# The second matrix of FFN 1 by the seven-product block scheme that FFN 2 already uses

## The chip, the core and the metric

The kernel runs on one core of a Trainium2 chip. A core has five engines that run side by side, each with its own instruction list: TensorE (PE, the matrix multiplier), VectorE (DVE), ScalarE (ACT), GpSimd (POOL) and SyncE (SP, which issues most DMA transfers). They wait for one another by semaphores. An engine executes its list strictly in the order written, so an instruction that waits also holds up everything behind it in its own list.

The metric is device time in microseconds (us) of one execution. Before the change three runs took 1120.14, 1120.99 and 1121.80 us, so the median is 1120.99 us. The profiled execution took 1119.95 us, of which its trace covers a span of 1118.2 us.

## The reference

The function is one layer of a hybrid streaming encoder for 512 tokens of width 1024, in fp32. Reduced to what matters:

```python
def swiglu(x, w1, w3, w2):
    return (jax.nn.silu(x @ w1) * (x @ w3)) @ w2      # w1, w3: 1024 x 2816, w2: 2816 x 1024

f = swiglu(rms_norm(h, pre_g1), w1a, w3a, w2a)        # FFN 1
h = h + 0.5 * rms_norm(f, post_g1)
u = rms_norm(h, mix_pre_g)                            # feeds attention, RG-LRU and gates
...
h = h + rms_norm(merged @ w_o, mix_post_g)
f = swiglu(rms_norm(h, pre_g2), w1b, w3b, w2b)        # FFN 2
h = h + 0.5 * rms_norm(f, post_g2)
```

The hidden width 2816 is 22 tiles of 128. "w2a" is the second matrix of FFN 1 and "w2b" that of FFN 2; the work here is the two products `hidden @ w2`, 512 x 2816 by 2816 x 1024.

## The kernel before

**Precision.** Every fp32 product is made of three passes of the multiplier over rounded parts: high times high, low times high and high times low. `split2` makes the two parts of a tile: ACT copies it to the rounded type (`whi` or the first half of `hT`), and DVE subtracts that copy from the original (`wlo`). So each weight tile and each hidden tile costs an ACT copy and a DVE subtraction before PE can use it. For some tiles DVE is spared: ACT writes the negated original into `wlo` and a DMA issued by POOL adds the same weights from memory to it (an "accumulate DMA").

**The order of work** is written out by hand. The Python program emits instructions for all engines in one sequence, and each engine's list is its part of that sequence. Weights are loaded and split in the order of the list `order`; `get`, `dma_to` and `split_to` advance along it. `later` and `point` emit small pieces of work at chosen places between matmuls. SBUF is handed out in 42 slots of 128 x 1024 fp32, PSUM in eight banks.

**FFN, first half.** The first tiles of the hidden width (four in FFN 1, two in FFN 2) are made one by one; tiles 2 and 3 of FFN 1 (`kept`) are stored raw and finished later by `gate_kept` (a DVE multiplication by `Rb` and an ACT silu) and `swiglu_kept`. The rest goes through `Pairs.run`: a job makes two tiles of `x @ w1` or `x @ w3` by seven block products instead of eight, `a11, s1, s2, a12 (by c11), s4, s3, a22` (in the last job a12 comes behind s3), each of 12 matmuls of 256 columns (`mm_s`). Between them ACT copies partial results out of PSUM (`q1`, `q5`, `u`, `v`) and DVE adds them. The last product `a22` of a job is emitted inside the next job, by `last()`. It accumulates in the same bank `bu` from which `v` is copied, so it can begin only when ACT has made that copy. For a w1 job of FFN 1 `last()` also multiplies the result by `Rb` on DVE, and ACT then applies silu. Towards the end of the last job two calls of `tail()` prepare the first w2 tiles, and two hooks `late[end, 1]` and `late[end, 2]` can place more work behind its first and second product.

**FFN 1, second half** (`tok_gemm`). Before, `w2a` is a plain product. For 15 of the 22 tiles each weight tile is used for all four groups of 128 tokens (24 matmuls of 512 columns a tile); the last 7 tiles (`RF`) are kept and used group by group, so that the norm of one group of tokens (`norms`, `post_norm`) runs beside the matmuls of the next.

**FFN 2, second half** (`Halves`). Tiles 0 to 15 of `w2b` go through seven block products `m1, m5, m2, m6, m7, m3, m4`, each summed over four groups of four tiles: 28 units, each of 12 matmuls of 512 columns. `prep(n)` prepares the operands of a unit: ACT copies (`whi`, and `hx` or `uT`), DVE subtractions for the low parts, and `sums` (`T` on weights, `S` on hidden tiles, both DVE) for the next product. `run` calls `prep` five units ahead (`LEAD`) of the unit that it emits, then calls the hooks of that unit, then emits the matmuls, and at the end of a product emits `out`, which copies the product out of PSUM: on ACT for m1, m5 and m6, as an addition on DVE for m7. The banks `bu` are used in turn by m1, m6, m7 and m4, so m7 can begin only when ACT has copied m6 out. The first four units are prepared inside the last pair job, by the two hooks and the two calls of `tail()`. The remaining six tiles, 16 to 21, go group by group as in FFN 1, and `post_norm` adds the stored partial results (`part`) with one DVE addition for each. `LO_DMA` names the units whose low weights come by accumulate DMA: two of m1 (groups 2 and 3) and all of m2; m3 always has them that way.

Of the kernel before, what the change touches and what calls it, by code (L numbers as in the profile page):

```python
# [15 lines left out]
P = 128  # L16
# [35 lines left out]
def hybrid_layer(ctx: ExitStack, tc: tile.TileContext, a: dict, out: bass.AP):  # L52
# [48 lines left out]

    order = []

    def want(name, n, first=0):
        order.extend((name, i) for i in range(first, n))

    paired = set()

# [6 lines left out]
            order.extend([(na, i), (na, i + 1), (nb, i), (nb, i + 1)])  # L115

    want_ffn("w1a", "w3a", NC1)
    want("w2a", FT)
    order += [("xr", i) for i in range(8)]
    order += [("wg", i) for i in range(8)]  # L120
    order += [("wk", 0), ("wk", 1), ("wv", 0), ("wv", 1)]
# [8 lines left out]
    paired.update(range(len(order), len(order) + 16 - WGP))  # L130
    order += [("wg", i) for i in range(WGP, 16)]
    order += [("wao", i) for i in range(8)]
    want("wo", 8)
    want_ffn("w1b", "w3b", NC2)
    want("w2b", FT, SF)

    st = {"dma": 0, "split": 0, "get": 0}
    raws, pairs = {}, {}
# [44 lines left out]
    def get(nm, i, ahead=2, rawahead=3):  # L183

        k = st["get"]
        assert order[k] == (nm, i), (order[k], nm, i)
        dma_to(k + 1 + ahead)
        split_to(k + 1 + ahead)
        dma_to(st["split"] + rawahead)
        st["get"] += 1  # L190
        return pairs.pop(k)
# [5 lines left out]
    def later(n, fn, rank=1):  # L197
        uid[0] += 1
        due.append((now[0] + n, rank, uid[0], fn))
# [36 lines left out]
    def mm_tok(acc, x, t, w, first, last, ns=(0, 1), skip=False):  # L236

        wh, wl = w
        c = slice(t * P, (t + 1) * P)
        for n in ns:  # L240
            s = slice(n * 512, (n + 1) * 512)
            pe.matmul(acc[n], x[:, 0, c], wh[:, s], start=first, stop=False, skip_group_check=skip)  # L242
            pe.matmul(acc[n], x[:, 0, c], wl[:, s], start=False, stop=False, skip_group_check=skip)  # L243
            pe.matmul(acc[n], x[:, 1, c], wh[:, s], start=False, stop=last, skip_group_check=skip)  # L244
# [66 lines left out]
            if after:  # L311
                after(n, c)

    def norms(acc, t, gpost, scale, gpre, spill, eps, mid=None):

        hg = slot([P, D], name="hg")
        junk = slot([P, D], name="junk")
        ss = small(2, "ss")
        rs = Rstd2()

        def half(n, c):
            act.activation(junk[:, c], h[t][:, c], AF.Square, accum_out=ss[:, n : n + 1])
            if n:
                rs.first(ss)
                dve.tensor_tensor(out=hg[:, c], in0=h[t][:, c], in1=gpre[:, c], op=ALU.mult)

        post_norm(acc, t, gpost, scale * NEWT, h[t], half, eps=eps, mid=mid)
        ht = h[t]
        if spill:
            sp.dma_start(out=h_scr[t], in_=h.pop(t))  # L330
        rs.root(ss)
        r = rs.value()
        dve.scalar_tensor_tensor(out=hg[:, :512], in0=ht[:, :512], scalar=r, in1=gpre[:, :512], op0=ALU.mult, op1=ALU.mult)
        act.activation(hg[:, 512:], hg[:, 512:], AF.Copy, scale=r)
        return hg
# [30 lines left out]
    def tok_gemm(nm, xs, n, R, gpost_name, scale, gpre_name, first, x_to=None, xf=None, spill=False, then=None, eps=None, pre=None):  # L366
# [8 lines left out]
        def accs(t):  # L375
            if t not in acc:
                acc[t] = [bank("acc"), bank("acc")]
            return acc[t]
# [21 lines left out]
                    if t % 2:  # L400
                        point()
        point(True)
        for k in range(F, n):
            x_to(k + 1)
            w[k] = get(nm, k, ahead=max(0, n - 1 - k), rawahead=2)
        gpost = bcast(gpost_name)
        gpre = bcast(gpre_name) if gpre_name else None
        if gpre_name:
# [4 lines left out]
        dma_to(st["split"] + 2)  # L413
        for t in range(NT):
            for ns in ((0,), (1,)):
                for k in range(F, n):
                    mm_tok(accs(t), xs[k], t, w[k], k == F if pre and t > 1 and ns == (1,) else k == 0, k == n - 1, ns, bool(pre))
            if not gpre_name:
                o = slot([P, D], name="o")

                def store(nn, c, t=t, o=o):
                    sp.dma_start(out=out[t * P : (t + 1) * P, c], in_=o[:, c])

                post_norm(acc[t], t, gpost, scale * NEWT, o, store, t == NT - 1, part=pre and pre.part(t))
                continue
            if t == NT - 1:
                break
            if t >= 1:
                trs[t - 1] = transpose_mm(us[t - 1])
            if t == NT - 2:  # L430

                transpose_out(trs[t - 1], t - 1)
            us[t] = norms(acc[t], t, gpost, scale, gpre, spill, ep(t))
            if t == 1:
                transpose_out(trs[t - 1], t - 1, xf)
        if not gpre_name:
# [16 lines left out]
        start(range(3))  # L453
        trs[t - 1] = transpose_mm(us[t - 1])
        mm_feat(bs[0], ws[0], 0, 256, ks=range(3, KT))
        us[t] = norms(acc[t], t, gpost, scale, gpre, spill, ep(t), between)
        transpose_out(trs[t - 1], t - 1, parts=(1,))
        transpose_xf(trs[t - 2], t - 2, xf, (1,))
        start()
# [30 lines left out]

    class Hidden:

        def __init__(self, block=0):
            self.f, self.t, self.done, self.block, self.eo = {}, {}, block, block, {}

        def place(self, f, own=None):

            if f >= self.block:
                return own
            g = f // 4  # L500
            if g not in self.eo:
                self.eo[g] = [slot([P, 2, SEQ], name="hEO") for _ in range(2)]
            return self.eo[g][f % 2][:, f // 2 % 2, :]

        def to(self, n):
            while self.done < n and self.done in self.f:
                hT = slot([P, 2, SEQ], F32R, name="hT")
                split2(hT[:, 0, :], hT[:, 1, :], self.f.pop(self.done))
                self.t[self.done] = hT
                self.done += 1  # L510

        def __getitem__(self, k):
# [2 lines left out]
    class Halves:  # L515
# [6 lines left out]

        def __init__(self, nm, hid, hooks):
            self.nm, self.hid, self.hooks = nm, hid, hooks
            self.gs = (1, 2, 3, 0)
            self.raw, self.ops, self.loaded, self.ready = {}, {}, 0, 0
            self.bank, self.c, self.accs, self.cast = {}, {}, {}, {}

# [104 lines left out]
        def run(self):  # L633
            for u in range(28):
                self.prep(u + LEAD)
                for fn in self.hooks.get(u, ()):
                    fn()
                self.unit(u)
                if u % 4 == 3 and self.NAMES[u // 4] in ("m1", "m5", "m6", "m7"):
                    later(0, lambda m=self.NAMES[u // 4]: self.out(m), 0)  # L640
                point()
            self.hid.eo.clear()
            for t in range(NT):
                n0 = self.bank["bc" if t < 2 else "bu"][t % 2]
                self.accs[t] = [n0, self.bank["bx"][t] if t < 2 else bank("acc")]
            self.bank.clear()

    QH = 4 * P

# [332 lines left out]
            load_x(2 * kp + 1)  # L982
    dma_to(NS + 2)

    hid, X1 = Hidden(), {}
    Rb = slot([P, 2, SEQ], name="Rb")
    pairs_a = Pairs(("w1a", "w3a"), NC1, FT, X1, hid, Rb)
    h_load([a["x"][t * P : (t + 1) * P, :] for t in range(NT)])
# [206 lines left out]
    for i in range(P // 16):  # L1195
        late[4 + i, 1] = [lambda i=i: bias_spread(i)]

    def w2_ahead():
        hid.to(hid.done + 1)
        split_to(st["split"] + 1)  # L1200

    pairs_a.run(w2_ahead, late)
    X1 = pairs_a = late = None
    for f in range(NG, NC1):
        later(1, lambda f=f: gate_kept(f))
        later(3, lambda f=f: swiglu_kept(f))
    later(10, softplus)
    xf = {(hh, th): slot([P, 4, 256], name="xf") for hh in range(2) for th in range(2)}
    bs = tok_gemm(
        "w2a", hid, FT, RF, "ffn1_post_g", 0.5, "mix_pre_g", [("xr", i) for i in range(4)], hid.to, xf=xf, spill=True, eps=veps)  # L1210
    hid = None


# [371 lines left out]
        mg.append(m)  # L1585


    hid, tn = Hidden(SF), []
    X2 = {"b11": uview(0, 0), "b21": uview(1, 0), "b22": uview(1, 1)}
    pairs_b = Pairs(("w1b", "w3b"), NC2, FT, X2, hid)  # L1590
    dma_one(pairs_b.k0)
# [27 lines left out]

    dve.tensor_tensor(out=tn[3], in0=xf[1, 0], in1=tn[1], op=ALU.subtract)  # L1620
    xf.clear()
    hid.f[0] = silu_mul(bs[0], bs[1], out=hid.place(0))
    X2["t3"] = to_slots(tn[2])
    hid.f[1] = silu_mul(bs[2], bs[3], out=hid.place(1))
    del bs
    late = {(0, 1): [lambda: X2.update(t4=to_uT(tn[3], 0, 1)), tn.clear]}
    pairs_b.prep(1, 1)

    def tail_tile(n):
        hid.to(n)  # L1630
        split_to(st["get"] + n - SF)

    def h_back(t):
        h[t] = slot([P, D], name="h")
        sp.dma_start(out=h[t], in_=h_scr[t])

    hooks = {u: [] for u in range(28)}
    for n, u in enumerate(RAW_TAIL):
        hooks[u].append(lambda n=n: dma_to(st["get"] + n + 1))
    for n, u in enumerate(SPLIT_TAIL):  # L1640
        hooks[u].append(lambda n=n: tail_tile(SF + n + 1))
    for t, u in enumerate(H_BACK):
        hooks[u].append(lambda t=t: h_back(t))
    half = Halves("w2b", hid, hooks)
    pairs_b.more = lambda n: half.load(LOAD_PAIRS[n])
    ahead = lambda: half.prep(half.ready + 1)
    end = len(pairs_b.jobs) - 1
    late[end, 1], late[end, 2] = [ahead], [ahead]
    pairs_b.run(ahead, late)
    X2 = pairs_b = None  # L1650
    tok_gemm("w2b", hid, FT, FT - SF, "ffn2_post_g", 0.5, None, [], hid.to, pre=half)


CONV_AT = (0, 1, 2, 4, 5, 6, 8, 10)
# [20 lines left out]
BY_DMA = {("wg", i) for i in range(2)}  # L1675

BY_POOL = {("wg", i) for i in range(2, 8)} | {("wk", 0), ("wk", 1)}
RF = 7

SF = 16  # L1680
LEAD = 5
U_SLOTS = 4
CAST_AT = 15
LO_DMA = {(m, i) for m in ("m1", "m2") for i in range(4)} - {("m1", 0), ("m1", 1)}
LOAD_PAIRS = (0, 4, 6, 8)
RAW_TAIL = (14, 16, 18, 20, 22, 24)
SPLIT_TAIL = (16, 18, 20, 22, 24, 26)
# [11 lines left out]
NG = 2  # L1699
# [55 lines left out]
```

## Time and profile before

| what | value |
|---|---|
| median of three runs | 1120.99 us (1120.14 to 1121.80) |
| profiled execution | 1119.95 us, span 1118.2 us |
| PE busy | 1107.4 us, 99 % of the span |
| DVE busy | 878.9 us, 79 % |
| ACT busy | 646.1 us, 58 % |
| `w2a` in FFN 1, plain | from 232.35 us to 353.9 us of the span |
| `w2b` blocks in FFN 2 | first matmul at 998.82 us |
| last matmul | starts at 1110.50 us |

All times inside the trace are counted from the start of the span. A timeline row gives the start, the duration, the engine, the line, the operation with what it writes and reads, and in brackets how long the engine was idle before it and what released it. Rows of the same kind that follow each other are joined ("x2"), and their duration is that of all together. A single matmul of 512 columns is listed with about 0.39 us because the rows include the pipeline's depth; consecutive ones start about 0.23 us apart, and that distance is what counts. The same holds for DVE and ACT: a row's start to the next row's start is what an instruction costs in a full queue. The granted clock (PEclk) is the share of full speed that the chip allowed the multiplier.

### The profile page before, as it was taken

What the parts mean: (1) busy time and instruction counts of PE and PEld (TensorE: products, weight loads), DVE (VectorE), ACT (ScalarE), POOL (GpSimd) and SP (SyncE); (2) the same over time, 40 slices, a digit from 0 to 9 for tenths busy, and PEclk for the clock granted to TensorE, in tenths of its full rate; (3) what the DMA queues carried; (4) which work ended last, traced back from release to release, by engine and by line L of the source; (5) the groups of instructions that cost most, each with busy time, mean ns of one, the idle gap of its engine ahead of it and who ended that gap; (6) DMA issues with size and microseconds to landing.
All of it is one profiled execution on the core that took longest, in us unless ns stands there. A gap on an engine that the chain in (4) does not pass through costs nothing.

```text
span 1118.2 us, 17951 instructions
## 1 busy us (share of the span) xinstructions
PE 1107.4 (99%) x6898; PEld 998.9 (89%) x6898; DVE 878.9 (79%) x1279; ACT 646.1 (58%) x1143; POOL 380.1 (34%) x298
## 2 busy tenths in 40 slices
PE   9999999999999999999999999999999999999997
PEld 7899999988888877899888888888999999997885
DVE  5899989887437978888678867767889899789944
ACT  7755555574326687756656564456455555577721
POOL 0044344200101523223556573010976665502100
PEclk9999999999999999999999999999999999999999
DMA  9226563264313553147223245342332323487732
GB/s 346 96 89 146 123 148 114 76 221 155 113 57 115 156 144 107 45 151 245 76 76 94 92 155 208 136 185 94 114 89 102 114 77 113 149 227 157 198 118 76
DMA packets 47319, 148.06 MB, mean 132 GB/s; under 512 B 5233, under 2 KB 7153, under 8 KB 47233
## 3 DMA queue, kind: packets, MB, share of 16 engines
q1 hardware_dynamic: 39632, 127.47, 33.7%
q0 software_dynamic: 7312, 18.92, 8.6%
q8 instruction: 54, 0.88, 0.3%
q10 hardware_dynamic: 288, 0.52, 0.2%
q14 instruction: 33, 0.26, 0.1%
HBM read 131.18 MB, written 13.62 MB: 129 GB/s over the span
## 4 chain that ended last, share of the span: by engine, by line
PE 98%; DMA 2%; DVE 0%; issue 0%; ACT 0%; DVEq 0%; SPq 0%; ACTq 0%
PE c L657 13%; PE c L658 13%; PE c L659 13%; PE f L224 9%; PE f L225 9%; PE f L226 9%; PE acc L243 5%; PE acc L242 5%; PE acc L244 5%; PE hw L613 2%; PE hw L614 2%; PE hw L612 2%; DMA wlo<-in_w2b_dram 1%; PE pt L1496 1%; PE hw L244 1%; PE hw L243 1%
## 5 line engine op out<-in xcount | busy, mean ns | idle before, releaser
L658 PE MATMUL c<-uT,wlo 128*128 128x256 f32 x516 | 146.0, 283 | 0.0
L659 PE MATMUL c<-uT,whi 128*128 128x256 f32 x516 | 146.0, 283 | 0.0
L657 PE MATMUL c<-uT,whi 128*128 128x256 f32 x516 | 146.0, 283 | 0.0
L658 PE MATMUL c<-Xh,wlo 128*128 128x256 f32 x504 | 142.7, 283 | 0.0
L657 PE MATMUL c<-Xh,whi 128*128 128x256 f32 x504 | 142.7, 283 | 0.0
L224 PE MATMUL f<-uT,whi 128*128 128x512 f32 (+1 forms) x368 | 136.4, 371 | 0.0
L225 PE MATMUL f<-uT,wlo 128*128 128x512 f32 (+1 forms) x368 | 134.8, 366 | 0.0
L226 PE MATMUL f<-uT,whi 128*128 128x512 f32 (+1 forms) x368 | 134.8, 366 | 0.0
L659 PE MATMUL c<-Xl,whi 128*128 128x256 f32 x456 | 129.0, 283 | 0.0
L214 DVE TENSOR_TENSOR wlo<-S,whi 128x1024 fp32r<-128x1024 f32 x86 | 120.1, 1396 | 6.5 <-POOL OL L1532 3.1
L213 ACT ACTIVATE whi<-S 128x1024 fp32r<-128x1024 f32 x86 | 88.3, 1054 | 23.1 <-DVE S L706 22.0
L658 PEld LDWEIGHTS c<-uT,wlo 128*128 128x128 f32 x516 | 99.0, 192 | 0.2
L657 PEld LDWEIGHTS c<-uT,whi 128*128 128x128 f32 x516 | 99.0, 192 | 0.2
L659 PEld LDWEIGHTS c<-uT,whi 128*128 128x128 f32 x516 | 99.0, 192 | 0.0
L657 PEld LDWEIGHTS c<-Xh,whi 128*128 128x128 f32 x504 | 96.8, 192 | 0.3 <-issue 0.3
L658 PEld LDWEIGHTS c<-Xh,wlo 128*128 128x128 f32 x504 | 96.7, 192 | 0.1
L659 PEld LDWEIGHTS c<-Xl,whi 128*128 128x128 f32 x456 | 87.5, 192 | 0.0
L224 PEld LDWEIGHTS f<-uT,whi 128*128 128x128 f32 x368 | 69.4, 189 | 12.5 <-issue 1.7
L226 PEld LDWEIGHTS f<-uT,whi 128*128 128x128 f32 x368 | 69.4, 188 | 11.4
L225 PEld LDWEIGHTS f<-uT,wlo 128*128 128x128 f32 x368 | 69.4, 189 | 10.8
L1480 POOL TENSOR_SCALAR P<-P,d 128x256 f32<-128x256 f32 (+1 forms) x64 | 62.5, 991 | 45.2 <-DVE d L1478 25.3
L242 PE MATMUL acc<-whi,hT 128*128 128x512 f32 x188 | 73.3, 390 | 0.0
(429 smaller groups left out, 3139.8 us busy)
## 6 DMA issues: line engine op xcount, KB each, us to landing
raw_w2a<-in_w2a_dram SPq DMA_DIRECT2D x22, 512.0 KB, 4.0
raw_w1b<-in_w1b_dram SPq DMA_DIRECT2D x22, 512.0 KB, 4.3
raw_w3b<-in_w3b_dram SPq DMA_DIRECT2D x22, 512.0 KB, 4.4
raw_w2b<-in_w2b_dram SPq DMA_DIRECT2D x22, 512.0 KB, 5.8
raw_w3a<-in_w3a_dram SPq DMA_DIRECT2D x21, 512.0 KB, 4.5
raw_w1a<-in_w1a_dram SPq DMA_DIRECT2D x20, 512.0 KB, 4.3
raw_wg<-in_wg_dram SPq DMA_DIRECT2D x16, 512.0 KB, 3.9
wlo<-in_w2b_dram POOLq DMA_DIRECT2D x10, 512.0 KB, 6.9
```

Of the source, the lines that this page charges most:

```text
L213: act.activation(hi, src, AF.Copy)
L214: dve.tensor_tensor(out=lo, in0=src, in1=f32(hi), op=ALU.subtract)
L224: pe.matmul(ps[:, c0:c1], wh[:, s], h_, start=k == 0 and c0 == 0, stop=False, skip_group_check=True)
L225: pe.matmul(ps[:, c0:c1], wl[:, s], h_, start=False, stop=False, skip_group_check=True)
L226: pe.matmul(ps[:, c0:c1], wh[:, s], l_, start=False, stop=k == KT - 1, skip_group_check=True)
L242: pe.matmul(acc[n], x[:, 0, c], wh[:, s], start=first, stop=False, skip_group_check=skip)
L243: pe.matmul(acc[n], x[:, 0, c], wl[:, s], start=False, stop=False, skip_group_check=skip)
L244: pe.matmul(acc[n], x[:, 1, c], wh[:, s], start=False, stop=last, skip_group_check=skip)
L657: pe.matmul(ps, wh[:, s], xh, start=first, stop=False, skip_group_check=True)
L658: pe.matmul(ps, wl[:, s], xh, start=False, stop=False, skip_group_check=True)
L659: pe.matmul(ps, wh[:, s], xl, start=False, stop=k == 3, skip_group_check=True)
L1480: pool.tensor_scalar(out=pt[:, x, b0:256], in0=pt[:, x, b0:256], scalar1=d[:, x : x + 1], scalar2=None, op0=ALU.mult)
```

## The change

`w2a` is now made by the same block scheme, and the setting up of that scheme moves from FFN 2 into a function `blocks` that both call. In both FFNs the 16 tiles in blocks are 4 to 19 (`gs = (1, 2, 3, 4)`), and the six others are `TAIL`. `LO_DMA` keeps only m2, so all low parts of m1 are now subtractions on DVE, in both FFNs. Three things of FFN 1 are fitted in: the gates of the two kept tiles become hooks of units 15, 17, 18 and 19 and stand first among the hooks of their unit; `softplus` becomes a hook of unit 25; and the residual `h`, so far held in four slots throughout FFN 1, is dropped and loaded again from `x` during the units named by `H_BACK`. `norms` passes the partial results on to `post_norm`. In FFN 2 tiles 0 and 1 go to a slot of their own.

```diff
-    want("w2a", FT)
+    want("w2a", TAIL)
...
-    want("w2b", FT, SF)
+    want("w2b", TAIL)
...
-            us[t] = norms(acc[t], t, gpost, scale, gpre, spill, ep(t))
+            us[t] = norms(acc[t], t, gpost, scale, gpre, spill, ep(t), part=pre and pre.part(t))
...
-            self.gs = (1, 2, 3, 0)
+            self.gs = (1, 2, 3, 4)
...
+    def blocks(nm, hid, pairs, late, h_src):
+
+        hooks = {u: [] for u in range(28)}
+
+        def tail_tile(n):
+            hid.to(n + 1)
+            split_to(st["get"] + n + 1)
+
+        def h_back(t):
+            h[t] = slot([P, D], name="h")
+            sp.dma_start(out=h[t], in_=h_src(t))
+
+        for at_, fn in ((RAW_TAIL, lambda n: dma_to(st["get"] + n + 1)), (SPLIT_TAIL, tail_tile), (H_BACK, h_back)):
+            for n, u in enumerate(at_):
+                hooks[u].append(lambda n=n, fn=fn: fn(n))
+        half = Halves(nm, hid, hooks)
+        pairs.more = lambda n: half.load(LOAD_PAIRS[n])
+        ahead = lambda: half.prep(half.ready + 1)
+        end = len(pairs.jobs) - 1
+        late[end, 1], late[end, 2] = [ahead], [ahead]
+        pairs.run(ahead, late)
+        return half
...
-    def w2_ahead():
-        hid.to(hid.done + 1)
-        split_to(st["split"] + 1)
-
-    pairs_a.run(w2_ahead, late)
+    h.clear()
+    half = blocks("w2a", hid, pairs_a, late, lambda t: a["x"][t * P : (t + 1) * P, :])
     X1 = pairs_a = late = None
-    for f in range(NG, NC1):
-        later(1, lambda f=f: gate_kept(f))
-        later(3, lambda f=f: swiglu_kept(f))
-    later(10, softplus)
+    for u, fn in zip(KEPT_AT, (gate_kept, swiglu_kept) * (NC1 - NG)):
+        half.hooks[u].insert(0, lambda f=NG + KEPT_AT.index(u) // 2, fn=fn: fn(f))
+    half.hooks[SOFTPLUS_AT].append(softplus)
...
-    tok_gemm("w2b", hid, FT, FT - SF, "ffn2_post_g", 0.5, None, [], hid.to, pre=half)
+    half = blocks("w2b", hid, pairs_b, late, lambda t: h_scr[t])
+    X2 = pairs_b = None
+    tok_gemm("w2b", hid, FT, len(TAIL), "ffn2_post_g", 0.5, None, [], pre=half)
...
-RF = 7
-
-SF = 16
+
+TAIL = (0, 1, 2, 3, 20, 21)
+KEPT_AT = (15, 17, 18, 19)
+SOFTPLUS_AT = 25
...
-LO_DMA = {(m, i) for m in ("m1", "m2") for i in range(4)} - {("m1", 0), ("m1", 1)}
+LO_DMA = {("m2", i) for i in range(4)}
```

More of the change, by code (lines that the diff above doesn't have):

```diff
@@ L102, in hybrid_layer, with want @@
     order = []
-    def want(name, n, first=0):
-        order.extend((name, i) for i in range(first, n))
+    def want(name, tiles):
+        order.extend((name, i) for i in tiles)
     paired = set()
@@ L132, in hybrid_layer @@
     order += [("wao", i) for i in range(8)]
-    want("wo", 8)
+    want("wo", range(8))
     want_ffn("w1b", "w3b", NC2)
-    want("w2b", FT, SF)
+    want("w2b", TAIL)
     st = {"dma": 0, "split": 0, "get": 0}
@@ L312, in post_norm, with norms @@
                 after(n, c)
-    def norms(acc, t, gpost, scale, gpre, spill, eps, mid=None):
+    def norms(acc, t, gpost, scale, gpre, spill, eps, mid=None, part=None):
         hg = slot([P, D], name="hg")
@@ L325, in half @@
                 dve.tensor_tensor(out=hg[:, c], in0=h[t][:, c], in1=gpre[:, c], op=ALU.mult)
-        post_norm(acc, t, gpost, scale * NEWT, h[t], half, eps=eps, mid=mid)
+        post_norm(acc, t, gpost, scale * NEWT, h[t], half, eps=eps, mid=mid, part=part)
         ht = h[t]
@@ L402, in tok_gemm @@
         point(True)
-        for k in range(F, n):
-            x_to(k + 1)
-            w[k] = get(nm, k, ahead=max(0, n - 1 - k), rawahead=2)
+        tail = list(pre.hid.seq) if pre else list(range(F, n))
+        for i, k in enumerate(tail):
+            x_to(F + i + 1)
+            w[k] = get(nm, k, ahead=max(0, len(tail) - 1 - i), rawahead=2)
         gpost = bcast(gpost_name)
@@ L415, in tok_gemm @@
             for ns in ((0,), (1,)):
-                for k in range(F, n):
-                    mm_tok(accs(t), xs[k], t, w[k], k == F if pre and t > 1 and ns == (1,) else k == 0, k == n - 1, ns, bool(pre))
+                for k in tail:
+                    new = k == tail[0] and (t > 1 and ns == (1,) if pre else k == 0)
+                    mm_tok(accs(t), xs[k], t, w[k], new, k == tail[-1], ns, bool(pre))
             if not gpre_name:
@@ L455, in tok_gemm @@
         mm_feat(bs[0], ws[0], 0, 256, ks=range(3, KT))
-        us[t] = norms(acc[t], t, gpost, scale, gpre, spill, ep(t), between)
+        us[t] = norms(acc[t], t, gpost, scale, gpre, spill, ep(t), between, pre and pre.part(t))
         transpose_out(trs[t - 1], t - 1, parts=(1,))
@@ L491, in hybrid_layer, with __init__ @@
     class Hidden:
-        def __init__(self, block=0):
-            self.f, self.t, self.done, self.block, self.eo = {}, {}, block, block, {}
+        def __init__(self, seq):
+            self.seq, self.f, self.t, self.done, self.eo = seq, {}, {}, 0, {}
         def place(self, f, own=None):
-            if f >= self.block:
+            if f in self.seq:
                 return own
@@ L505, in to @@
         def to(self, n):
-            while self.done < n and self.done in self.f:
+            while self.done < min(n, len(self.seq)) and self.seq[self.done] in self.f:
+                k = self.seq[self.done]
                 hT = slot([P, 2, SEQ], F32R, name="hT")
-                split2(hT[:, 0, :], hT[:, 1, :], self.f.pop(self.done))
-                self.t[self.done] = hT
+                split2(hT[:, 0, :], hT[:, 1, :], self.f.pop(k))
+                self.t[k] = hT
                 self.done += 1
@@ L983, in hybrid_layer @@
     dma_to(NS + 2)
-    hid, X1 = Hidden(), {}
+    hid, X1 = Hidden(TAIL), {}
     Rb = slot([P, 2, SEQ], name="Rb")
@@ L1196, in hybrid_layer @@
         late[4 + i, 1] = [lambda i=i: bias_spread(i)]
-    def w2_ahead():
-        hid.to(hid.done + 1)
-        split_to(st["split"] + 1)
-    pairs_a.run(w2_ahead, late)
+    h.clear()
+    half = blocks("w2a", hid, pairs_a, late, lambda t: a["x"][t * P : (t + 1) * P, :])
     X1 = pairs_a = late = None
-    for f in range(NG, NC1):
-        later(1, lambda f=f: gate_kept(f))
-        later(3, lambda f=f: swiglu_kept(f))
-    later(10, softplus)
+    for u, fn in zip(KEPT_AT, (gate_kept, swiglu_kept) * (NC1 - NG)):
+        half.hooks[u].insert(0, lambda f=NG + KEPT_AT.index(u) // 2, fn=fn: fn(f))
+    half.hooks[SOFTPLUS_AT].append(softplus)
     xf = {(hh, th): slot([P, 4, 256], name="xf") for hh in range(2) for th in range(2)}
     bs = tok_gemm(
-        "w2a", hid, FT, RF, "ffn1_post_g", 0.5, "mix_pre_g", [("xr", i) for i in range(4)], hid.to, xf=xf, spill=True, eps=veps)
+        "w2a", hid, FT, len(TAIL), "ffn1_post_g", 0.5, "mix_pre_g", [("xr", i) for i in range(4)], xf=xf, spill=True, eps=veps, pre=half)
+    half = None
     hid = None
@@ L1585, in mg_out @@
         mg.append(m)
-    hid, tn = Hidden(SF), []
+    hid, tn = Hidden(TAIL), []
     X2 = {"b11": uview(0, 0), "b21": uview(1, 0), "b22": uview(1, 1)}
@@ L1621, in hybrid_layer @@
     xf.clear()
-    hid.f[0] = silu_mul(bs[0], bs[1], out=hid.place(0))
+    t01 = slot([P, 2, SEQ], name="sw")
+    hid.f[0] = silu_mul(bs[0], bs[1], out=t01[:, 0, :])
     X2["t3"] = to_slots(tn[2])
-    hid.f[1] = silu_mul(bs[2], bs[3], out=hid.place(1))
+    hid.f[1] = silu_mul(bs[2], bs[3], out=t01[:, 1, :])
+    del t01
     del bs
@@ L1627, in hybrid_layer @@
     pairs_b.prep(1, 1)
[L1629 to L1649, printed above, removed]
+    half = blocks("w2b", hid, pairs_b, late, lambda t: h_scr[t])
     X2 = pairs_b = None
-    tok_gemm("w2b", hid, FT, FT - SF, "ffn2_post_g", 0.5, None, [], hid.to, pre=half)
+    tok_gemm("w2b", hid, FT, len(TAIL), "ffn2_post_g", 0.5, None, [], pre=half)
 CONV_AT = (0, 1, 2, 4, 5, 6, 8, 10)
```

## The prediction

> **What bounds the kernel now.** I read the page's busy shares and clock first, then PE's waits, then the timelines of the stages that the change touches.
>
> ```profile
> span 1118.2 us, 17951 instructions
> ...
> PE 1107.4 (99%) x6898; PEld 998.9 (89%) x6898; DVE 878.9 (79%) x1279; ACT 646.1 (58%) x1143; POOL 380.1 (34%) x298
> ...
> PEclk9999999999999999999999999999999999999999
> ```
>
> ```profile
> PE hw L613 <- DMA wlo<-in_w2b_dram: 2.0, 2, 1.1
> ```
>
> PE is busy 99% of the span at full clock and hardly waits; past its first microseconds its only waits are two on low weights in FFN 2's m1. A matmul removed is time saved, and every new wait of PE is time lost. Two things set the price of a matmul, and two the block scheme's pace. The chain that ended last shows the first:
>
> ```profile
> 334.06 0.23 PE acc L242
> ...
> 343.60 0.87 PE tr L343 x8
> ```
>
> Between these rows lie one group's 7 tail tiles x 2 halves x 3 = 42 matmuls of 512 columns: 9.54 / 42 = 0.227 us each, so a unit of 12 takes 2.73.
>
> **1. Matmuls removed.** Plain, 16 tiles of `w2a` take 16 x 24 = 384; in blocks 28 x 12 = 336. Saved: 48 x 0.227 = 10.9 us, all on PE's path. Tail: 6 x 24 in both.
>
> **2. The last pair job of FFN 1: a new wait (stall A).** PE, then ACT, then DVE there:
>
> ```profile
> 230.91 0.28 PE L657 MATMUL c<-Xh,w 128*128 128x256 f32 x1
> ...
> 232.35 0.40 PE L242 MATMUL acc<-whi,hT 128*128 128x512 f32 x1
> ```
> ```profile
> 225.35 0.38 ACT L796 ACTIVATE cc<-c 128x256 f32<-128x256 f32 x1 [1.06 <-PE c L659]
> 226.79 0.38 ACT L756 ACTIVATE ct<-c 128x256 f32<-128x256 f32 x1 [1.06 <-PE c L659]
> 227.07 1.05 ACT L798 ACTIVATE cc<-cc 128x1024 f32<-128x1024 f32 x1
> 228.02 0.62 ACT L213 ACTIVATE hT<-sw 128x512 fp32r<-128x512 f32 x1
> 228.54 1.05 ACT L178 ACTIVATE whi<-raw_w2a 128x1024 fp32r<-128x1024 f32 x1
> 229.67 0.39 ACT L778 ACTIVATE ct<-c 128x256 f32<-128x256 f32 x1
> ```
> ```profile
> 221.97 0.69 DVE L214 TENSOR_TENSOR w<-raw_w3a,w 128x512 fp32r<-128x512 f32 x1
> 225.77 1.23 DVE L797 TENSOR_TENSOR cc<-cc,Rb 128x1024 f32<-128x1024 f32 x1 [3.11 <-ACT cc L796]
> ```
>
> The hooks behind a11 and s1 now put units 0 and 1 on ACT and DVE, ahead of `last()`'s multiplication by Rb (L797). What a unit of m1 costs DVE is shown by FFN 2:
>
> ```profile
> 990.30 1.23 DVE L593 TENSOR_TENSOR wlo<-raw_w2b,whi 128x1024 fp32r<-128x1024 f32 x1 [1.17 <-ACT whi L588]
> 991.44 0.69 DVE L214 TENSOR_TENSOR hx<-hEO,hx 128x512 fp32r<-128x512 f32 x1
> 992.05 1.22 DVE L545 TENSOR_TENSOR raw_w2b<-raw_w2b,raw_w2b 128x1024 f32<-128x1024 f32 x1
> ...
> 993.78 1.22 DVE L593 TENSOR_TENSOR wlo<-raw_w2b,whi 128x1024 fp32r<-128x1024 f32 x1
> ```
>
> That is 993.78 - 990.30 = 3.48 us a unit, 1.14 for 1024 wide operations and 0.60 for 512. DVE begins unit 0 when its first copy, behind q1's, is there, about 223.8. Two units end at 230.8, and the multiplication at 232.0, where it used to end at 227.0. ACT's silu (L798) waits for it, and behind the silu in ACT's list stand unit 2's two copies (0.95 and 0.5 by the distances above) and only then the copy of `v` (L778): 232.1 + 0.95 + 0.95 + 0.5 = 234.5, done at 234.9. PE's last a22 accumulates into the bank that `v` is copied from, so it starts at 234.9, not 230.9. Stall A: 4.0 us. From the spread of the terms I allow 3.3 to 4.7. Before, the 3.11 us of DVE idle there covered the step.
>
> **3. DVE after that.** Unit 2 on DVE waits for its copy (234.1); units 2 and 3 and six small additions of the job end at 243.5, where unit 4 begins (234.1 + 2 x 3.48 + 2.4; four of the six take the 1.73 between the first two rows below, the other two 0.33 each). In FFN 2:
>
> ```profile
> 1002.60 0.41 DVE L767 TENSOR_TENSOR cc<-c,ct 128x256 f32<-128x256 f32 x1
> ...
> 1004.33 1.21 DVE L593 TENSOR_TENSOR wlo<-raw_w2b,whi 128x1024 fp32r<-128x1024 f32 x1
> ...
> 1048.44 0.69 DVE L214 TENSOR_TENSOR uT<-hEO,uT 128x512 fp32r<-128x512 f32 x1
> ```
> ```profile
> 1020.00:1040.00 20.00, 20.00 (x90) 16.54 (x89) 20.00 (x27) 14.98 (x21) 5.27 (x6) 1.00 0.84 189
> ```
>
> DVE (third of the busy columns) never rests there: 44.1 us from unit 4's first subtraction to the end of unit 19's `T`. In FFN 1 that ends at 243.5 + 44.1 = 287.6. PE starts unit 0 at 232.4 + 4.0 = 236.4 and would reach unit 16 at 236.4 + 16 x 2.73 = 280.0. By the same operations a unit of m5 costs DVE 3.48, of m2 and m6 2.34, of m7 2.87, which is 4 x 11.03 = 44.1 again; so counted, operands stay just ahead of PE up to unit 15, closest at unit 8 (0.2 us).
>
> **4. The kept gate at unit 15 (stall B).** These rows ran beside plain matmuls before:
>
> ```profile
> 237.16 1.28 DVE L1164 TENSOR_TENSOR kept<-kept,Rb 128x512 f32<-128x512 f32 x2
> ...
> 237.88 1.24 ACT L1165 ACTIVATE kept<-kept 128x512 f32<-128x512 f32 x2 [4.46 <-DVE kept L1164]
> ```
>
> (The second is ACT's.) Now the hook of unit 15 runs after `prep` of unit 19, so the DVE multiplication stands behind unit 19's `T`: 287.6 + 0.64 = 288.25. ACT's silu waits for it (0.62, to 288.9), and ACT's copy of m6 out of `bu` is emitted behind unit 15, thus behind that silu. Unit 16 (m7) begins in the same bank:
>
> ```profile
> 1044.48 1.28 ACT L626 ACTIVATE hc<-hw 128x512 f32<-128x512 f32 x2 [3.40 <-PE hw L614]
> ```
>
> In FFN 2 this copy waited for PE alone. In FFN 1 its first half ends near 289.5, 9.5 us after PE is ready. Lower end: with DVE as far ahead as in FFN 2 (1048.44 against m6's end near 1044.5 + 0.5), 3.4 + 0.64 + 0.62 + 0.64 = 5.3; upper 10.5. I take 9.5, the sum by this stage's own times. The gates at 18 and 19 meet a DVE that has then caught up: nothing.
>
> **5. The clock after stall B.**
>
> ```profile
> 1110.00:1111.00 1.00, 0.89 (x4) 0.39 (x3) 0.08 (x1) 0.00 (x0) 0.00 (x0) 1.00 0.00 0
> ...
> 1115.00:1116.00 1.00, 0.00 (x0) 0.00 (x0) 0.21 (x1) 0.00 (x0) 0.00 (x0) 0.91 0.73 280
> 1116.00:1118.20 2.20, 0.00 (x0) 0.00 (x0) 0.00 (x0) 0.00 (x0) 0.00 (x0) 0.50 0.32 111
> ```
> ```profile
> 1.10 4.21 PE L964 MATMUL w<-warm 128*128 128x256 f32 x18 [1.10 <-POOL warm L961]
> 5.63 0.80 PE L1014 MATMUL f<-uT,whi 128*128 128x512 f32 x1 [0.33 <-ACT uT L1007]
> ```
>
> After the last matmul (about 1110.9) the granted clock, the column before the DMA share, holds at 1.00 until about 1115.8 and is 0.50 from then: 4.9 us of idle. At the start 256-column matmuls come 4.21 / 18 = 0.234 us apart, twice the 0.12 of the pair jobs (1.44 for the 12 between the PE rows of part 2), and the slow pace lasts through the 0.80 matmul, to about 6.4: 5.3 us at half speed, 2.6 lost. Stall B, 9.5, is past 4.9, so PE should restart at half clock. The price lies between 0 (it holds) and 2.6; I take 2.6, the one restart shown. Stall A, 4.0, is short of it: 0.
>
> The Trainium skill ("TensorE: Matmul & The Clock Gate", Part 1: The HAM clock gate) says that the clock halves after at least one idle window of about 3.4 us and is restored after a busy one of the same length. That agrees with a drop seen after 4.9; by its window the restart would lose 3.4 / 2 = 1.7 (an estimate from that page), and the sum would be 0.9 lower. By its rule a gap of 4.0 could halve the clock too, which is rival (c).
>
> **6. The rest of FFN 1.** POOL's accumulate DMAs of m2 and m3 are queued behind one another and land as in FFN 2:
>
> ```profile
> wlo<-in_w2b_dram POOLq DMA_DIRECT2D x10, 512.0 KB, 6.9
> ```
>
> Unit 8's is issued behind ACT's copies of m1 (unit 3 ends at 236.4 + 10.9 = 247.3) and two copies of 0.95, at about 250.2, and is needed at 236.4 + 8 x 2.73 = 258.2: 1.1 us of cover at the median. I take 0; a landing later than that costs PE the excess. SP's extra loads (16 half-tiles instead of tiles, and four of `h`) wait for nothing that PE needs soon: 0. The norm of the last group of tokens gains `part`'s addition on its path, 0.69 at the most (the 512-wide rows of DVE); rows of before for its end and for the transposes that need it:
>
> ```profile
> 359.35 0.72 ACT L334 ACTIVATE hg<-hg,r 128x512 f32<-128x512 f32 x1 [0.61 <-DVE r L264]
> ```
> ```profile
> 360.98 0.87 PE tr L343 x8
> ```
>
> It was done at 360.07, 0.9 before PE came to it, so 0.69 more is covered: 0. If that slack is gone the price is the 0.69, and the earlier groups, with 6 x 0.227 = 1.4 less matmul time beside them, could add a little: 0 to 1. `softplus` and the kept products lie on engines with room: 0.
>
> **7. FFN 2.** The waits for m1's accumulate DMAs go:
>
> ```profile
> 998.82 0.40 PE L612 MATMUL hw<-whi,hx 128*128 128x512 f32 x1
> ...
> 1005.62 0.50 PE L613 MATMUL hw<-wlo,hx 128*128 128x512 f32 x1 [0.95 <-DMA wlo<-in_w2b_dram]
> ...
> 1009.70 0.50 PE L613 MATMUL hw<-wlo,hx 128*128 128x512 f32 x1 [1.06 <-DMA wlo<-in_w2b_dram]
> ...
> 1012.33 0.39 PE L612 MATMUL hw<-whi,uT 128*128 128x512 f32 x1
> ```
>
> m1's 48 matmuls should take 10.9 and took 13.5: 2.6 gained. But DVE, full, gets two more subtractions, 2 x 1.14 = 2.28. Unit 7's operands would be ready at 1004.33 + 2.28 + 3 x 3.48 + 1.74 = 1018.8 and PE, without stalls, is there at 1009.7 + 3 x 2.73 = 1017.9: 0.8 late. Gain 1.8 (0 to 2.6).
>
> **Sum.** -10.9 + 4.0 + 9.5 + 2.6 - 1.8 = +3.4. The profiled execution, 1119.95 (span 1118.2 and 1.75 around it), becomes 1123.4. It lies 1.0 below the median 1120.99, on which the sum gives 1124.4, my forecast.
>
> **Rivals.** (a) *Faster*: DVE reaches unit 19 in time, and stall B vanishes. Its place is the end of `prep` 19, 287.6 by my count. For it: half the count is carried over from FFN 2. Against it: FFN 2's DVE, with less to do, was still at unit 19's `T` 3.4 us after m6's end. Then -10.9 + 4.0 - 1.8 = -8.7: 1112.3. It decides (faster by over 0.2%, 2.24 us, which is about what a measurement here can tell) when stall B with its clock is under 6.5 us. (b) *Both stalls, but the clock holds* or recovers at once: +0.8, 1121.8. For it: no row shows a halved clock after a gap inside the kernel. (c) *The clock falls after stall A too*, or a DMA or norm is late: +2.6 more, 1127.0. For it: the drop after 4.9 does not show that less would not do. Against it: nothing shows that it would. (d) *Neither stall*: -12.7, 1108.3; it needs ACT free of both silus, which the written order forbids.
>
> **How the numbers follow.** Forecast 0.50 (its own range 1122.5 to 1126.5), (a) 0.15, (b) 0.20, (c) 0.13, (d) 0.02. The range 1117 to 1128 leaves out (a), (d) and part of (c). It is what the bounds make it: all terms at their lower ends give -10.9 + 3.3 + 5.3 - 2.6 = -4.9, 1116.1; at their upper ends, with one clock loss, -10.9 + 4.7 + 10.5 + 2.6 + 1.0 = +7.9, 1128.9. Faster: (a), (d) and the low end of (b), 0.02: 0.19. Within 0.2%: most of (b), 0.16, and 0.04 of the forecast: 0.20. Slower: 0.61.
>
> **What would show it.** Right: PE idle about 4 us before an a22 matmul near 231, released by the ACT copy of `v`; about 9.5 us near 280, released by ACT's copy out of m6; ACT's kept silu there released by the DVE multiplication; granted clock below 1 right behind it; no wait on `wlo` DMAs in FFN 2's m1, but a short one on DVE at unit 7. Wrong: no gap at 280, DVE idle in 243 to 288, or waits on m2's DMAs at unit 8.

## The result and the profile after

The changed kernel takes 1122.89 us (median of 11 runs, 1121.94 to 1123.66) against 1120.43 us before (11 runs, 1119.43 to 1121.80): a ratio of 1.0021, with a 95% interval of 1.0012 to 1.0030. It is 2.5 us slower. The prediction was 1124.4 us, 3.4 us slower, with a range of 1117 to 1128. The profiled execution took 1123.3 us.

The page of the changed kernel shows 48 matmuls fewer and DVE busier, and two dips of PE and of its granted clock that were not there before:

```profile
span 1121.5 us, 17990 instructions
...
PE 1101.1 (98%) x6850; PEld 993.1 (89%) x6850; DVE 914.2 (82%) x1337; ACT 669.2 (60%) x1175; POOL 390.0 (35%) x308
...
PE   9999999989799999999999999999999999999997
...
PEclk9999999989899999999999999999999999999999
```

PE's waits name both stalls. The waits for FFN 2's DMAs are gone:

```profile
PE hw L615 <- ACT hc L629: 7.0, 1, 7.0
PE c L683 <- ACT ct L804: 3.8, 1, 3.8
PE w L990 <- POOL warm L987: 1.1, 1, 1.1
PE f L1040 <- ACT uT L1033: 0.6, 1, 0.6
```

**Stall A**, in the last pair job of FFN 1. DVE's timeline, ACT's and PE's (L804 is the copy of `v`, L823 the product with Rb, L824 its silu):

```profile
229.74 0.69 DVE L551 TENSOR_TENSOR hEO<-hEO,hEO 128x512 f32<-128x512 f32 x1
230.34 1.22 DVE L823 TENSOR_TENSOR cc<-cc,Rb 128x1024 f32<-128x1024 f32 x1
233.62 1.23 DVE L596 TENSOR_TENSOR wlo<-raw_w2a,whi 128x1024 fp32r<-128x1024 f32 x1 [2.07 <-ACT whi L591]
```
```profile
231.59 1.06 ACT L824 ACTIVATE cc<-cc 128x1024 f32<-128x1024 f32 x1 [4.19 <-DVE cc L823]
232.55 1.04 ACT L591 ACTIVATE whi<-raw_w2a 128x1024 fp32r<-128x1024 f32 x1
233.50 0.61 ACT L213 ACTIVATE hx<-hEO 128x512 fp32r<-128x512 f32 x1
234.02 0.36 ACT L804 ACTIVATE ct<-c 128x256 f32<-128x256 f32 x1
```
```profile
234.43 0.58 PE L683 MATMUL c<-Xh,w 128*128 128x256 f32 x1 [3.82 <-ACT ct L804]
```

The row that used to be at 230.91 is at 234.43, behind the two units on DVE, the product, the silu, two copies of unit 2 and the copy of `v`, in that order.

**Stall B**, before unit 16. The chain that ended last passes there from DVE to ACT to PE (start, length, what):

```profile
286.03 1.14 DVE raw_w2a L548
287.17 0.61 DVE kept L1190
...
287.81 0.05 ACT kept L1191
...
288.34 0.59 ACT hc L629
...
288.97 0.80 PE hw L615
```

L548 is unit 19's `T`, L1190 and L1191 are the gate of the kept tile, L629 the copy of m6. PE's previous matmul had started at 281.63.

**The clock.** The column before the DMA share is the granted clock, in windows of half a microsecond of the changed kernel:

```profile
230.50:231.00 0.50, 0.12 (x2) 0.00 (x0) 0.50 (x1) 0.00 (x0) 0.00 (x0) 1.00 0.46 131
...
232.50:233.00 0.50, 0.00 (x0) 0.00 (x0) 0.00 (x0) 0.50 (x2) 0.00 (x0) 0.80 0.14 49
...
239.50:240.00 0.50, 0.50 (x3) 0.39 (x3) 0.50 (x2) 0.00 (x0) 0.00 (x0) 0.88 1.03 385
```
```profile
282.00:282.50 0.50, 0.01 (x1) 0.00 (x0) 0.50 (x2) 0.00 (x0) 0.00 (x0) 1.00 0.45 180
283.50:284.00 0.50, 0.00 (x0) 0.00 (x0) 0.50 (x1) 0.00 (x0) 0.00 (x0) 0.99 0.00 0
284.00:284.50 0.50, 0.00 (x0) 0.00 (x0) 0.50 (x2) 0.00 (x0) 0.00 (x0) 0.50 0.71 90
...
294.00:294.50 0.50, 0.50 (x4) 0.36 (x3) 0.50 (x2) 0.50 (x1) 0.50 (x1) 0.77 1.00 184
```

It fell to half in both gaps, about 2 us after PE stopped, and came back about 5 us after PE went on. PE's rows give the price. Behind A, the 12 matmuls of a22 and the first six of unit 0 took 5.25 us (234.43 to 239.68) where the pace of before makes them 12 x 0.12 + 6 x 0.227 = 2.80: 2.4 lost. Behind B, unit 16 took 5.29 us (288.97 to 294.26) and not 2.73: 2.6 lost. The rows with which the full pace begins:

```profile
239.68 0.40 PE L615 MATMUL hw<-whi,hx 128*128 128x512 f32 x1
```
```profile
294.26 0.40 PE L615 MATMUL hw<-whi,uT 128*128 128x512 f32 x1
```

Both prices are those of the profiled execution. Its mean granted clock over the span is 0.990, as in two others of the eleven runs; in the other eight it is 0.993 or 0.994, the values of e2 and e3 below, in whose profiles only B halved the clock. So in most runs A probably cost no half clock, or less of it; their traces were not kept.

**FFN 2.** From the first block matmul to the last matmul of all it was 998.82 to 1110.50 = 111.68 us before and is 1003.85 to 1113.53 = 109.68 now. m1 has no waits; unit 7, predicted 0.8 late, is 0.7 late (3.43 us for a unit of 2.72), by two short pauses:

```profile
1022.94 0.39 PE L615 MATMUL hw<-whi,uT 128*128 128x512 f32 x1
1023.33 0.50 PE L616 MATMUL hw<-wlo,uT 128*128 128x512 f32 x1
1023.94 0.50 PE L617 MATMUL hw<-whi,uT 128*128 128x512 f32 x1
1024.28 0.40 PE L615 MATMUL hw<-whi,uT 128*128 128x512 f32 x1
```

| term, us | predicted | in the trace |
|---|---|---|
| 48 matmuls fewer | -10.9 | -10.9 |
| stall A | +4.0 | +3.8 |
| half clock after A | 0 | +2.4 |
| stall B | +9.5 | +7.0 |
| half clock after B | +2.6 | +2.6 |
| FFN 2 | -1.8 | -2.0 |
| rest (spans 1118.2 to 1121.5, less the above) | 0 | +0.4 |
| sum | +3.4 | +3.3 |

### The profile page after: what moved, and what is told of

It reads as the page before. It is cut to its first block, busy times and chain, and to the rows that moved or that the text cites. A ratio compares the mean times of both kernels' runs of the same rounds, so it can differ in the third digit from the quotient of the medians.

```text
span 1121.5 us, 17990 instructions
## 1 busy us (share of the span) xinstructions
PE 1101.1 (98%) x6850; PEld 993.1 (89%) x6850; DVE 914.2 (82%) x1337; ACT 669.2 (60%) x1175; POOL 390.0 (35%) x308
## 4 chain that ended last, share of the span: by engine, by line
PE 93%; DVE 5%; ACT 1%; issue 1%; DMA 0%; DVEq 0%; SPq 0%; ACTq 0%
PE c L683 13%; PE c L684 13%; PE c L685 13%; PE f L224 9%; PE f L225 9%; PE f L226 9%; PE hw L615 4%; PE hw L617 4%; PE hw L616 4%; PE acc L244 2%; PE acc L242 2%; PE acc L243 2%; PE hw L243 1%; PE hw L244 1%; PE hw L242 1%; DVE wlo L596 1%
## 5 line engine op out<-in xcount | busy, mean ns | idle before, releaser
L615 PE MATMUL hw<-whi,uT 128*128 128x512 f32 x192 | 76.0, 396 | 7.0 <-ACT hc L629 7.0
L224 PEld LDWEIGHTS f<-uT,whi 128*128 128x128 f32 x368 | 69.4, 189 | 12.7 <-issue 1.4
```

Of the source, the lines that this page charges most:

```text
L224: pe.matmul(ps[:, c0:c1], wh[:, s], h_, start=k == 0 and c0 == 0, stop=False, skip_group_check=True)
L615: pe.matmul(ps, xs[:, 0, j, c], hi[:, j, :], start=start and j == 0, stop=False, skip_group_check=True)
```

## The experiments

The medians below have a kernel before of their own, run beside them: 1120.75 us for the first four, 1120.48 us for the last four (18 runs each). The theory was that of the prediction, with one addition read from the chain: **stall B ends when DVE is done with unit 19 and the gate, at about 289, whenever PE gets there.** Then what PE loses before it, at A and by A's half clock, is lost only once. The rival was that the stalls add up.

**e1: stall B taken away.** The gates stand at later units, behind the copy of m6.

```diff
-KEPT_AT = (15, 17, 18, 19)
+KEPT_AT = (18, 19, 20, 21)
```

> The kept gates move from units 15, 17, 18, 19 to units 18 to 21 of FFN 1, behind the copy of m6 out of its bank. Theory (stall B is the ACT copy held behind the kept silu): the 6.96 us wait shrinks to the copy's own 0.6 us and the 2.7 us of half clock behind it go: 1122.9 - 6.4 - 2.7 = about 1113.8; stall A stays at 3.8. Rival (DVE is the bound there anyway, and unit 16 onwards would wait for its operands): at most 3 us gained, 1120.

Measured: 1117.30 us (1115.98 to 1118.35), ratio to before 0.9969 (0.9958 to 0.9980). PE's waits:

```profile
PE c L683 <- ACT ct L804: 3.8, 1, 3.8
...
PE hw L243 <- DVE wlo L179: 0.6, 1, 0.6
PE tr L343 <- DVE hg L333: 0.5, 1, 0.5
```

Stall B is gone, A is as it was, and the kernel is 5.6 us below the changed one, not 9.1. From the first block matmul to the last transposes of FFN 1 the two traces differ by 7.35 us (237.16 to 365.76 against 239.54 to 360.79); the two new small waits in the tail take 1.1 of what is missing. The rest lies ahead of the change's place: this profile reached its first block matmul 2.4 us later, because its start went on at half pace for longer (below). That the six runs scatter over 2.4 us fits that, but it fits A's half clock as well: the three runs near 1118.3, the profiled one among them, have a mean granted clock of 0.995, the three near 1116.3 one of 0.996. Which of the two it is, and so how much of the 5.6 is luck, stays open.

**e2: stall A taken away, DVE left as it was.** In the last job, silu and the preparation of unit 2 are emitted behind the copy of `v`.

```diff
-                if n == len(self.jobs) - 1:
+                if n == len(self.jobs) - 1 and self.R is None:
                     silu()
                     silu = lambda: None
                     tail()
...
+                late_silu = n == len(self.jobs) - 1 and self.R is not None
-                silu()
-                silu = lambda: None
+                if not late_silu:
+                    silu()
+                    silu = lambda: None
                 mm_s(W["s3"], X["t3"], bu, True)
...
                 act.activation(v, bu, AF.Copy)
+                if late_silu:
+                    silu()
+                    silu = lambda: None
+                    tail()
```

> In the last pair job of FFN 1, ACT's silu and the preparation of unit 2 move behind the copy of v. DVE's order stays but for two small additions (0.66 us). Theory (stall B ends when DVE has finished unit 19 and the gate, whenever PE gets there, so it absorbs what PE loses at A): stall A and its half clock vanish, 3.8 + 2.4 = 6.2, but the wait at unit 16 grows from 7.0 to 12.5, and the time falls by 0.7 at most: 1122.2. Rival (the two stalls add up): 6.2 us gained, 1116.7.

Measured: 1124.14 us (1122.74 to 1125.38), ratio 1.0029 (1.0018 to 1.0040): nothing gained.

```profile
244.10 0.50 PE L616 MATMUL hw<-wlo,uT 128*128 128x512 f32 x1 [0.72 <-DVE wlo L596]
```
```profile
288.82 0.80 PE L615 MATMUL hw<-whi,uT 128*128 128x512 f32 x1 [9.37 <-ACT hc L629]
```

PE started unit 0 at 232.08 and not at 237.16, and unit 16 at 288.82 and not at 288.97. The 6.2 us won (5.1 at the start of unit 0, the rest in its first matmuls, now at full pace) were given back: 3.6 in units 4 to 7, which had to wait for DVE (the first of these pauses is shown; the four units took 14.5 us and not 10.9), and 2.4 in a longer stall B, 9.4. The stall was expected at 12.5 because the waits in m5 were not foreseen, but the sum is that of absorption, and the rival's 1116.7 is excluded.

**e3: the product with Rb ahead of unit 1 on DVE.** This takes A away and also the 2.07 us for which DVE stood idle behind it.

```diff
-        late[end, 1], late[end, 2] = [ahead], [ahead]
+        late[end, 1], late[end, 2 if pairs.R is None else 3] = [ahead], [ahead]
```

> In the last pair job of FFN 1, unit 1's preparation moves from behind the second product to behind the third, so DVE's multiplication by Rb stands ahead of it. Theory (absorption): stall A falls from 3.8 to about 0.4 and its half clock goes, but only the 2.1 us that DVE stood idle waiting for unit 2's ACT copy move the end of stall B: 1122.9 - 2.1 = 1120.8. Rival (stalls add): 5.8 plus up to 2 gained, 1115 to 1117.

Measured: 1121.60 us (1120.42 to 1123.43), ratio 1.0008 (0.9999 to 1.0017), 1.3 below the changed kernel. PE:

```profile
231.14 0.39 PE L683 MATMUL c<-Xh,w 128*128 128x256 f32 x1 [0.34 <-ACT ct L804]
```
```profile
286.99 0.80 PE L615 MATMUL hw<-whi,uT 128*128 128x512 f32 x1 [9.40 <-ACT hc L629]
```

A is 0.34 us. The end of stall B moved by 1.98 us, about as far as DVE had been idle, and not by the 5.6 that PE had won at unit 1 (235.41 and not 241.05). The median fell by 1.3 and not by the 2.1 expected; in this profile the half clock behind B lasted longer (6.2 us and not 5.3), which takes back 0.5.

**e4: e1 and e3 together.**

> e3 and e1 together. Theory: no stall A, no stall B, no half clock; DVE then limits units 8 to 12 a little (about 1.6 us) and m6's copy costs 0.6: 1122.9 - 6.2 - 9.7 + 2.2 = about 1109.2. Rival (another wait, the accumulate DMAs of m2 or m3 or DVE, takes most of it): no better than 1113.

Measured: 1114.21 us (1113.75 to 1114.42), ratio 0.9941 (0.9928 to 0.9953). Without B, the fix of A is worth 3.1 us by the medians (e1 to e4); with B it was worth 1.3. The expected 1109.2 was not reached. Part of the missing 5.0 us are waits that came up, 3.2 us in these lines:

```profile
PE hw L243 <- DVE wlo L179: 1.6, 1, 1.6
PE hw L616 <- DMA wlo<-in_w2a_dram: 1.2, 2, 0.9
...
PE tr L343 <- DVE hg L333: 0.4, 1, 0.4
```

For two of these e4's timelines suggest a cause, which e7 and e8 try. The split of the last tail tile stood behind softplus's small DVE operations (310.1 to 315.4), and the low parts of m3 behind a silu of a kept tile for which ACT waited:

```profile
289.09 0.63 ACT L1191 ACTIVATE kept<-kept 128x512 f32<-128x512 f32 x1 [5.24 <-DVE kept L1190]
```

**e5: the kernel before, with all of m1's low parts by DVE.**

```diff
-LO_DMA = {(m, i) for m in ("m1", "m2") for i in range(4)} - {("m1", 0), ("m1", 1)}
+LO_DMA = {("m2", i) for i in range(4)}
```

> The kernel before with one edit: all of m1's low parts by DVE, in FFN 2, the only place that has blocks there. Theory (the part on FFN 2 is worth what the two traces show, 111.68 against 109.68 us from the first block matmul to the last of all): 2.0 us faster, ratio 0.9982. Rival (the DMA waits return as DVE waits): ratio 1.000.

Measured: 1117.94 us (1117.39 to 1118.59), ratio 0.9974 (0.9963 to 0.9984). The gain, 2.5 us by the medians (1.8 to 4.1 by the interval), holds the 2.0 of the traces. So this part of the change is a gain by itself, and by difference the FFN 1 part costs some 5 us.

**e6: the clock kept up through stall B.** 28 matmuls into an unused bank, ahead of unit 16; nothing reads them.

```diff
+            if u == 16 and self.nm == "w2a":
+                warm = bank("warm")
+                for _ in range(28):
+                    pe.matmul(warm, self.last[0], self.last[1], start=True, stop=True, skip_group_check=True)
             if start:
                 self.bank[key] = [bank("hw") for _ in range(2)]
             hi, lo, xs = self.ops.pop(u)
+            self.last = xs[:, 0, 0, 0:P], hi[:, 0, :]
```

> The changed kernel with 28 extra matmuls of 512 columns into an unused bank ahead of unit 16 of FFN 1, 6.4 us of multiplying inside the 7.0 us wait; their result is read by nothing. Theory (12 matmuls behind stall B ran at half clock because PE had been idle): the granted clock stays at 1 there, the wait left is about 0.6, and the time falls by 2.7 to 1120.2. Rival (the slow pace is due to operands or to the wait itself): nothing gained, or 6.4 lost if the wait follows PE.

Measured: 1120.80 us (1120.49 to 1121.14), ratio 1.0000 (0.9991 to 1.0009), 2.1 below the changed kernel.

```profile
281.80 6.51 PE L612 MATMUL warm<-whi,uT 128*128 128x512 f32 x28
288.79 0.50 PE L620 MATMUL hw<-whi,uT 128*128 128x512 f32 x1 [0.48 <-ACT hc L634]
```
```profile
285.00:290.00 5.00, 4.52 (x20) 3.44 (x19) 2.58 (x4) 2.38 (x4) 0.00 (x0) 1.00 0.32 105
```

Unit 16 began at the same time as before (288.79 against 288.97), the granted clock stayed at 1.00, and the next unit began at 291.68 rather than 294.26, 2.6 us sooner. The slow pace behind the stall is the clock, caused by the idle, and its price in the changed kernel's profile is shown. These runs also bear out absorption: four have a mean granted clock of 0.995, like the profiled one, in which A still halved the clock, and seven one of 0.997, thus some 4.5 us less at half clock (0.002 x 1119 x 2); yet the median of either group is 1120.8.

**e7: softplus behind the last split** (on top of e4).

```diff
-SOFTPLUS_AT = 25
+SOFTPLUS_AT = 27
```

> e4 with softplus as the hook of unit 27 rather than 25, behind the last tail tile's split. In e4 its small DVE operations, 310.1 to 315.4, stood ahead of that split, and PE waited 1.6 us for it. Theory: that wait goes, 1114.2 - 1.6 = 1112.6. Rival (the small operations then delay the first norm by as much): 1114.2.

Measured: 1114.31 us (1114.09 to 1115.62), ratio 0.9946 (0.9933 to 0.9958): the rival was right. The wait only moved to the first norm:

```profile
PE tr L343 <- DVE hg L333: 2.7, 1, 2.7
```

**e8: the kept gates in the pair jobs** (on top of e7). Product, silu and product of each kept tile become hooks of jobs 11 to 16, one step to a job, so that ACT does not wait for DVE.

```diff
+    for i, f in enumerate(range(NG, NC1)):
+        for j, fn in enumerate((gate_kept, silu_kept, swiglu_kept)):
+            late[11 + 2 * j + i, 3] = [lambda f=f, fn=fn: fn(f)]
...
-    for u, fn in zip(KEPT_AT, (gate_kept, swiglu_kept) * (NC1 - NG)):
-        half.hooks[u].insert(0, lambda f=NG + KEPT_AT.index(u) // 2, fn=fn: fn(f))
```

> e7 with the kept gates (product with Rb, silu, product) as hooks of pair jobs 11 to 16 of FFN 1, where DVE has idle time, rather than of units 18 to 21. Theory: ACT's silu no longer holds up the low copies of m3 (5.2 us of ACT idle in e4), so the two waits on m3's accumulate DMA, 1.2 us with their consequences 1.6, go as well: about 1111. Rival (the gates lengthen the pair jobs through DVE or ACT): no better than e7.

Measured: 1112.88 us (1112.58 to 1113.42), ratio 0.9930 (0.9918 to 0.9943). This is the fastest version, 7.6 us below the kernel before and 10.0 below the changed one. It is faster than e7, but not for the reason given: the wait for m3's accumulate DMAs did not go.

```profile
PE hw L616 <- DMA wlo<-in_w2a_dram: 2.0, 2, 1.7
```
```profile
290.00:295.00 5.00, 4.77 (x22) 3.62 (x21) 5.00 (x7) 5.00 (x8) 0.00 (x0) 1.00 1.10 256
295.00:300.00 5.00, 3.43 (x15) 2.31 (x13) 5.00 (x7) 4.33 (x6) 0.00 (x0) 1.00 1.04 270
```

The last of these DMAs was issued at 287.4, five microseconds sooner than in e4 (292.4), and still came late, 12.7 us after its issue and not 6.0 as in e4: the DMA engines were fully busy from 285 (share 1.0 or more). What went is the 2.7 us wait at the first norm; whether other transfers in the same stretch delay these four was not tried.

## Why the prediction was right, and where a step was not

The outcome, slower by a little, came from the terms that were forecast, at the places forecast.

- **Parts 2 and 3 held to a few tenths.** The order of instructions on ACT and DVE, priced with rows of FFN 2, gave a22 at 234.9 (234.43) and the end of DVE's unit 19 plus the gate at 288.25 (287.78 in the chain). The claim that operands would stay just ahead of PE up to unit 15 was true here, with PE late by A and its half clock; without A it failed: in e2 units 4 to 7 lost 3.6 us to such waits, in e3 two of them about 1.1.
- **Part 4 had the end of stall B right and its length wrong:** it ended at 288.97, forecast 289.5, but began at 282.0, forecast 280.0. Length 7.0, not 9.5.
- **Part 5 failed in one step: "Stall A, 4.0, is short of it: 0."** One drop after 4.9 us at the end of the kernel was read as the time that a drop needs. In the changed kernel's profile the clock fell 2.2 us after PE stopped at A and 2.0 us after it stopped at B, and A's half clock cost 2.4. Two microseconds are no threshold either: in e2 the clock fell after 2.6 us of idle, in e3 after 5.4. The traces' clock records (when the granted clock changed, and to what) point to the reason. In them each stretch at half clock between two full ones lasts 6.83 or 10.24 us, and the full one between A and B 44.37: 2, 3 and 13 times 3.41. So in these runs the clock seems to change only in steps of 3.41 us, and where a gap falls among the steps decides when, and perhaps whether, it drops.
- **The other half of part 5, 2.6 for the restart behind B, was right in kind, as e6 showed, and met its size by luck.** Behind B the half pace lasted 5.3 us in the changed kernel, but 3.5 in e2 and 6.2 in e3, which makes the price 1.7 to 3.1.
- **The errors of A's half clock and of B's length cancel, and not by chance.** A's half clock makes PE arrive later at a point that DVE sets. So rival (c) was wrong too, in its price: in the profiled run its condition came true, and the time did not rise by 2.6. The same holds for stall A as a whole, as e2 showed. In the sum of part 4 the start of B should have been left open and its end fixed.
- **Part 7** forecast 1.8; the traces give 2.0 and e5 2.5 between the medians.
- **Part 6** was right: no wait for m2's DMAs, the norms covered. With the stalls gone (e4, e7, e8) that cover is used up, and the tail's split, the norm and m3's DMAs show as waits of 0.4 to 2.7 us.
- Rival (a), no stall B, is what e1 makes by moving the gates behind m6's copy, and the kernel is then faster than before, though at 1117.30 and not that rival's 1112.3: with B gone, A's half clock and two small waits count. In the changed kernel DVE had no chance to be in time, being busy without a pause from 243 to 287.7.

The Trainium skill ("TensorE: Matmul & The Clock Gate", Part 1: The HAM clock gate) gives at least one idle window of about 3.4 us as the condition for half rate and a busy one for full rate, and calls the window free-running. The steps of 3.41 us agree with a free-running window. That the window must be idle as a whole does not agree: the clock fell after 2.0 and 2.2 us of idle, so the window of 3.41 that ended there still held matmuls. From the restart to the full pace it took 3.5 to 6.2 us here, which agrees with one whole busy window behind a part of another. By its rule the 3.8 us of stall A could halve the clock, which it did in the profiled run.

## What to carry to other kernels

When a wait ends at a time that another engine sets, whatever is lost or won before it on the waiting engine does not count as long as some of that wait is left; sum such a path by end times on the engine that sets them, not by adding stalls. A hook that makes an engine wait belongs behind every copy that frees a bank, and one operation that waits for a fully loaded engine costs the whole backlog of that engine. After taking one wait away, look for the small ones that it had covered.

## What the runs showed of the hardware

The kernel's start is not the same in every execution. PE warms up with 18 matmuls. Behind them the real ones of 512 columns ran at full pace, 0.23 us apart but for short pauses, in the changed kernel's profile, and at half pace, 0.43 us apart, until 10.4 us in e1's (timelines of PE, the first of the changed kernel, the second of e1):

```profile
5.39 0.50 PE L1040 MATMUL f<-uT,whi 128*128 128x512 f32 x1 [0.57 <-ACT uT L1033]
5.73 0.40 PE L1041 MATMUL f<-uT,wlo 128*128 128x512 f32 x1
...
6.52 0.40 PE L1040 MATMUL f<-uT,whi 128*128 128x512 f32 x1
6.75 0.39 PE L1041 MATMUL f<-uT,wlo 128*128 128x512 f32 x1
```
```profile
9.94 0.63 PE L1040 MATMUL f<-uT,whi 128*128 128x512 f32 x1
10.37 0.50 PE L1041 MATMUL f<-uT,wlo 128*128 128x512 f32 x1
10.71 0.39 PE L1042 MATMUL f<-uT,whi 128*128 128x512 f32 x1
```

The profile prints the granted clock as 1.00 in both stretches, but the trace's clock record begins only at 4.1 us in the changed kernel and at 10.6 us in e1, where the full pace begins; before that only the distance of the matmuls shows the pace. Between these two profiles the start is worth 2.4 us, as much as the whole effect of this change.
